# Hybrid mLSTM / neighbourhood-attention encoder: absorbed factors gathered per head, first two tiles transposed in the projection's loop, three column blocks behind the mLSTM

## The chip, the cores and the metric

The kernel runs on one core of a Trainium2 chip. The metric is the device time of one execution in microseconds (us). Engines are named as in the profile: PE is TensorE (PEld its weight loads), DVE is VectorE, ACT is ScalarE, POOL is GpSimd, SP is SyncE, which here only issues DMAs. Each engine works through its own queue in order; a waiting instruction holds up what is queued behind it on that engine.

## The reference

One encoder layer on 1024 tokens of width 1024, all in float32, with three residual sub-layers. It is cut here to what the changed stages compute.

```python
ALPHA = 2 ** 0.25
h = layer_norm(x, ln_in_w, ln_in_b)

# (1) token mixer: bidirectional mLSTM (4 heads x 128) beside neighbourhood attention (8 heads x 64)
z = h @ w_in + b_in
y = concat([mlstm(z), neighbourhood_attention(z)])
h = layer_norm(ALPHA * h + y @ w_mix_out + b_mix_out, ln1_w, ln1_b)

# (2) cross-attention, 4 heads of 256, into 256 memory tokens
q = h @ w_q;  k, v = split(mem @ w_kv)
p = softmax(q_head @ k_head.T / 16)          # per head
h = layer_norm(ALPHA * h + concat(p @ v_head) @ w_o + b_o, ln2_w, ln2_b)

# (3) ConvFFN: up-projection, width-3 depthwise conv, GELU gate, down-projection
h = layer_norm(ALPHA * h + conv_ffn(h), ln3_w, ln3_b)
```

## The kernel before

The program is written in Python against a tile library: tiles come from pools in on-chip memory, a pool that closes hands its room to the next one, and the library adds all waits between engines. A planner orders the instructions of each engine from its own forecast of durations: what stands earlier in the program goes first if it is ready, and later work is pulled forward into gaps. The order so found is fixed at build time. `tc.issue_after(x)` keeps an instruction behind `x` on its engine. Float32 products are done as three products of split operands (`mm3`, lines 223 to 225): a high and a low part, either `fp32r` (`split`, lines 228 and 229) or scaled `f16` (`split16`, lines 202 and 203). Every weight therefore passes a raw buffer (tag `wraw`, two buffers), a high part by ACT (tag `whi`, five buffers) and a low part by DVE or POOL (tag `wlo`, five buffers).

The stages, in order, with the lines and names that matter below:

- **Token projection** (`tok_chunk`), in the pools `w1` and `survey`.
- **Memory projection and absorbed factors** (pool `mem`, lines 486 to 560). The transposed memory is loaded in two halves through `wraw` and split into `memTh` and `memTl`; 16 weight pieces (line 126) give `xk` and `xv`. Then the query weights are multiplied into the keys and the output weights into the values, head by head, so that cross-attention needs no query and no output projection: `kq` = w_q times k, `vo` = v times w_o. The stream `wq` loads two weight rows of 512 KB per head, 16 in all, two ahead. Even ones are split by ACT and DVE, odd ones by ACT (line 136) and POOL (lines 137 and 138). Each head's result is four blocks of 128 x 512 in PSUM; `stage` evicts one (lines 202 and 203) into one of four small tiles and stores its high and its low half by one transfer each (line 533).
- **Column blocks** (`col_gen`): 16 weight pieces times two halves of the tokens, 24 matmuls each. The first 16 blocks run ahead of the mLSTM.
- **mLSTM** (`ml_gen`), eight chunks. The other 16 blocks (the queries and keys of neighbourhood attention) are mixed into it: `mix` runs `ml_gen`, adds up the costs that it yields, and takes the next filler while the filler's share done is below the main part's. The call is `mix(tc, anchor, ml_gen(), 48.3, cg, 15, 3)`: the main part's total, the filler's total, and a lag of three steps. One block is taken ahead of the call. The tokens' transposes lie in `X1` (first half) and `X2`, and blocks read both.
- **Neighbourhood attention** (`na_gen`), with the first half of the output projection (`out_half`, tiles named `fill`) as its filler. The mLSTM's result comes back through `wraw` (line 811) and is split into `X1`; the attention's goes into `X2`.
- **Second half of the output projection** (`out_half` with bank `out`, pool `wkB`), eight tiles of 128 tokens in order 0 to 7. After each, `after1` does the layer norm (`ln_tile`), and the tile is stored to `h1_d`. In `ln_tile` a tile's statistics are held behind the previous tile's product with the norm's weight (line 254).
- **Cross-attention** (pool `wkC`): tiles in the order `todo` = 0, 2, 1, 3, 4, 6, 5, 7 are loaded again (`load_r`), transposed (`to_hT`, line 1073) and split into `h1T`; then `scores`, softmax, `to_PT`, `out_d` and the norm. `to_B` transposes the result for the ConvFFN; `evict_wb` scales it out of PSUM, half on ACT (line 955), half on DVE (line 957).
- **ConvFFN**: 22 units of up-projection, convolution and gate, then the down-projection.

Of the kernel before, what the change touches and what calls it, by code (L numbers as in the profile page):

```python
# [20 lines left out]
NT = 8  # L21
# [35 lines left out]
def encoder(ctx, tc, I, out):  # L57
# [73 lines left out]
    def wload16(src, a, b, s, pool=False):  # L131
        raw = wp.tile([128, WP], F32, name="wraw", tag="wraw", bufs=2)[:, :a * b]
# [147 lines left out]
    with ExitStack() as ca:  # L280

        yml = None
        with ExitStack() as cm:
# [202 lines left out]
            with ExitStack() as c2:  # L486
                mm = c2.enter_context(tc.tile_pool(name="mem", bufs=1, reuse_waits="tile"))
                mT = [mm.tile([128, 8, 256], F32R, name="memT" + n) for n in "hl"]
                for q in range(2):
                    raw = wp.tile([128, WP], F32, name="wraw", tag="wraw", bufs=2)[:, :1024].rearrange(  # L490
                        "p (k t) -> p k t", k=4)
                    S.dma_start(raw, I["memT"][:, q * 1024:(q + 1) * 1024].rearrange("p (k t) -> p k t", k=4))
                    split(*(m[:, 4 * q:4 * q + 4, :] for m in mT), raw)
# [10 lines left out]
                for j, name in enumerate(("xk", "xv")):  # L504
                    x = mm.tile([128, 8, 256], F32, name=name)
                    xs_.append(x)
                    for i in range(8):
# [13 lines left out]
                        if j == 1 and i > 1:  # L521
                            next(gg, None)

                wq = Stream([(I["w_xqT"][i * 128:i * 128 + 128], 1, 1024) for i in range(8)] +
                            [(I["w_xo"][i * 128:i * 128 + 128], 1, 1024) for i in range(8)], 2,
                            load=lambda a, b, c, e: wload16(a, b, c, swq if wq.n < 8 else sx, wq.n % 2))

                def stage(ps, dst, shape):
                    st = mm.tile([128, 2, 512], F16, name="stage", tag="stage", bufs=4)

                    split16(st[:, 0], st[:, 1], ps, 2.0 ** -23)
                    for n in range(2):
                        S.dma_start(dst(n), st[:, n].rearrange("p (a m) -> p a m", a=shape))

                for h in range(4):
                    w = [wq.get(2 * h), wq.get(2 * h + 1)]
                    xh, xl = pairs["xk"]
                    for j in range(4):
# [6 lines left out]
                        stage(ps, lambda n: kq_d[n, :, 2 * j:2 * j + 2, h * 256:h * 256 + 256], 2)  # L545
# [3 lines left out]
                for h in range(4):  # L549
                    w = [wq.get(8 + 2 * h), wq.get(9 + 2 * h)]  # L550
                    xh, xl = pairs["xv"]
                    for b in range(2):
                        m = slice(b * 128, b * 128 + 128)
                        for ch in range(2):
# [5 lines left out]
                            stage(ps, lambda n: vo_d[n, :, 2 * h + b:2 * h + b + 1, c], 1)  # L560
# [208 lines left out]
        def out_half(w, y, res, dst, work, name, after=None, bias=None, rbufs=3, early=False, alpha=ALPHA):  # L769
# [10 lines left out]

            load_r(0)
            yield 0
            for tt in range(NT):
                if tt + 1 < NT:
                    load_r(tt + 1)
                r = rs.pop(tt)
# [815 lines left out]
```

## Time and profile before

| | |
|---|---|
| median of 3 runs | 1666.44 us (1665.78 to 1666.67) |
| profiled execution | 1660.96 us, span 1659.2 us |
| busy share of the span | PE 91%, PEld 59%, DVE 58%, ACT 44%, POOL 35% |
| mean granted PE clock | 0.969 |
| DMA | 214.11 MB, mean 129 GB/s |

The span reaches from the first to the last instruction. In a row of the profile stand start, duration, engine, line of the kernel, operation, the tile written, an arrow and the tiles read, the shape and the count; brackets at its end give the idle time of the engine just before, and what ended it. Window rows give the busy time of each engine in a stretch of the span, then the clock granted to PE (1.00 is full speed) and the share of time in which the DMA engines were busy.

### The profile page before, as it was taken

How to read it: one execution, taken by the hardware profiler on the slowest of the kernel's cores; microseconds unless marked ns; L12 is line 12 of the kernel's file. 1: busy time of each engine (PE TensorE's matmuls, PEld its weight loads, DVE VectorE, ACT ScalarE, POOL GpSimd, SP SyncE). 2: the span in 40 equal slices, each digit the busy share in tenths (PEclk: the TensorE clock that was granted, in tenths of full speed). 3: DMA queues.
4: the chain of work that ended last, by engine and by line, in shares of the span. 5: the costliest groups of instructions: out<-in, count | busy, mean ns of one | idle time of the engine just before them, and what ended most of it. 6: DMA issues, size and time to landing. Idle time of an engine off the chain costs nothing.

```text
span 1659.2 us, 21607 instructions
## 1 busy us (share of the span) xinstructions
PE 1504.0 (91%) x8134; PEld 973.1 (59%) x8134; DVE 969.2 (58%) x1774; ACT 734.7 (44%) x1212; POOL 584.3 (35%) x389
## 2 busy tenths in 40 slices
PE   6999786799999589895999988999999999998998
PEld 6999774488888478784455543444444444443443
DVE  8433374213454568856345677878888886945333
ACT  3311354312443356641233456777777775712000
POOL 5312234521433357615111236444443430110443
PEclk9999898999999799997999999999999999999999
DMA  8254446521545464266000133233322241932121
GB/s 306 92 176 147 157 136 216 203 71 45 138 160 135 155 222 129 77 229 254 25 31 34 52 114 130 102 115 121 120 102 114 111 169 70 332 130 68 47 77 51
DMA packets 85384, 214.11 MB, mean 129 GB/s; under 512 B 8224, under 2 KB 33056, under 8 KB 81952
## 3 DMA queue, kind: packets, MB, share of 16 engines
q1 hardware_dynamic: 84992, 211.98, 36.8%
q8 instruction: 64, 1.05, 0.3%
q0 software_dynamic: 144, 0.49, 0.1%
q14 instruction: 40, 0.33, 0.1%
q10 hardware_dynamic: 144, 0.26, 0.0%
HBM read 161.75 MB, written 51.45 MB: 128 GB/s over the span
## 4 chain that ended last, share of the span: by engine, by line
PE 29%; DVE 11%; ACT 6%; DMA 3%; issue 1%; POOL 1%; SPq 0%; DVEq 0%; ACTq 0%
PE dn L224 5%; PE dn L225 5%; PE dn L223 5%; PE S L223 3%; PE S L224 3%; PE S L225 3%; DMA sv<-in_w_down_dram 3%; DVE cbuf L1299 2%; DVE cbuf L1300 2%; PE z L224 1%; PE z L225 1%; PE z L223 1%; ACT cbuf L1298 1%; ACT cbuf L1306 1%; DVE wlo L203 1%
## 5 line engine op out<-in xcount | busy, mean ns | idle before, releaser
L128 POOL TENSOR_TENSOR wlo<-wraw,whi 128x1024 fp32r<-128x1024 f32 (+1 forms) x38 | 91.3, 2407 | 198.9 <-ACT whi L127 176.0
L223 PE MATMUL dn<-whi,yp 128*128 128x512 f16 x336 | 126.9, 380 | 1.4 <-ACT whi L202 1.4
L224 PE MATMUL dn<-wlo,yp 128*128 128x512 f16 x336 | 127.7, 381 | 0.0
L225 PE MATMUL dn<-whi,yp 128*128 128x512 f16 x336 | 127.5, 380 | 0.0
L127 ACT ACTIVATE whi<-wraw 128x1024 fp32r<-128x1024 f32 (+1 forms) x52 | 54.9, 1060 | 148.8 <-PE tk L225 47.9
L1217 POOL TENSOR_TENSOR wraw<-ur 128x512 f32<-128x512 f32 x22 | 46.0, 2091 | 200.7 <-issue 187.4
L1299 DVE SCALAR_TENSOR_TENSOR cbuf<-C,wdw,cbuf 128x1024 f32<-128x1024 f32 x44 | 75.7, 1721 | 28.4 <-ACT cbuf L1298 28.3
L251 ACT ACTIVATE r<-r,lnrs 128x1024 f32<-128x1024 f32 x19 | 23.6, 1241 | 121.6 <-DVE lnrs L250 121.6
L1300 DVE SCALAR_TENSOR_TENSOR cbuf<-C,wdw,cbuf 128x1024 f32<-128x1024 f32 x44 | 70.5, 1602 | 1.2
L223 PE MATMUL S<-kq,h1T 128*128 128x512 f16 x128 | 49.5, 387 | 22.6 <-ACT h1T L202 22.6
L223 PEld LDWEIGHTS <-yp 128*128 128x128 f16 x352 | 34.5, 98 | 51.4 <-issue 10.4
L203 DVE SCALAR_TENSOR_TENSOR wlo<-wraw,sc,whi 128x1024 f16<-128x1024 f32 x29 | 43.5, 1521 | 31.4 <-ACT whi L202 31.3
L224 PEld LDWEIGHTS <-yp 128*128 128x128 f16 x352 | 34.6, 98 | 41.9 <-issue 0.8
L225 PEld LDWEIGHTS <-yp 128*128 128x128 f16 x352 | 34.5, 98 | 41.9 <-issue 0.8
L1298 ACT ACTIVATE cbuf<-C,bdw,wdw 128x1024 f32<-128x1024 f32 x44 | 54.5, 1238 | 10.0 <-DVE C L1335 9.0
L1075 POOL TENSOR_TENSOR r<-r,vec 128x1024 f32<-128x1024 f32 x8 | 18.8, 2348 | 113.1 <-PE tp L1073 113.1
L202 ACT ACTIVATE whi<-wraw,sc 128x1024 f16<-128x1024 f32 x29 | 32.4, 1142 | 58.6 <-PE dn L225 33.3
L223 PE MATMUL tk<-whi,X1h 128*128 128x256 f32 (+1 forms) x192 | 55.9, 292 | 1.6 <-DVE ev L335 0.6
L223 PE MATMUL tk<-whi,X2h 128*128 128x256 f32 (+1 forms) x192 | 54.7, 285 | 1.4 <-DVE V L330 1.4
L225 PE MATMUL tk<-whi,X1l 128*128 128x256 f32 (+1 forms) x192 | 55.4, 290 | 0.4 <-DVE lnrs L240 0.4
L224 PE MATMUL tk<-wlo,X1h 128*128 128x256 f32 (+1 forms) x192 | 55.3, 289 | 0.0
L225 PE MATMUL tk<-whi,X2l 128*128 128x256 f32 (+1 forms) x192 | 54.7, 285 | 0.0
(449 smaller groups left out, 4866.4 us busy)
## 6 DMA issues: line engine op xcount, KB each, us to landing
ur<-in_w_up_dram SPq DMA_DIRECT2D x22, 1024.0 KB
sv<-in_w_down_dram SPq DMA_DIRECT2D x22, 512.0 KB
y<-cbuf SPq DMA_DIRECT2D x22, 512.0 KB
ur<-y SPq DMA_DIRECT2D x11, 1024.0 KB
wraw<-in_w_down_dram SPq DMA_DIRECT2D x22, 512.0 KB
r<-h SPq DMA_DIRECT2D x19, 512.0 KB
wraw<-in_w_col_dram SPq DMA_DIRECT2D x16, 512.0 KB
h<-r SPq DMA_DIRECT2D x16, 512.0 KB
```

The source lines that it names most:

```text
L127: A.activation(hi[:, :n], r3, AF.Copy)
L128: (eng or G).tensor_tensor(lo[:, :n], r3, hi[:, :n].bitcast(F32), OP.subtract)
L202: A.activation(hi, src, AF.Copy, scale=s)
L203: return V.scalar_tensor_tensor(lo, src, s, hi, op0=OP.mult, op1=OP.subtract)
L223: T.matmul(ps, lh, rh, start=first, stop=False, skip_group_check=skip)
L224: T.matmul(ps, lh, rl, start=False, stop=False, skip_group_check=skip)
L225: return T.matmul(ps, ll, rh, start=False, stop=last, skip_group_check=skip)
L251: A.activation(r, r, AF.Identity, scale=rs[:, 0:1], bias=rs[:, 1:2])
L1217: G.tensor_tensor(S1, A21, A22, OP.add)
L1298: A.activation(c, C[:, 1:SEQ + 1], AF.Identity, scale=wdw[:, 1, j:j + 1], bias=bdw[:, j:j + 1])
L1299: V.scalar_tensor_tensor(c, C[:, 0:SEQ], wdw[:, 0, j:j + 1], c, op0=OP.mult, op1=OP.add)
L1300: V.scalar_tensor_tensor(c, C[:, 2:SEQ + 2], wdw[:, 2, j:j + 1], c, op0=OP.mult, op1=OP.add)
```

## The change

It has five parts.

1. The memory is loaded by one transfer of 1 MB into a tile of its own, which takes the slot of `xv`. Odd rows of `wq` get raw tiles of their own (`wr`, two buffers). `stage` becomes one tile per head with both halves of all four blocks, in the slots of `memTh` and `memTl` by turns; `evict` fills it, and two transfers of 512 KB store it.
2. The divisor of the filler in `mix` goes from 15 to 12.
3. `out_half` takes an order of tiles, and the second half uses `todo`. The pool `wkC` opens ahead of the loop, and `to_hT` is called in `after1`: for the first tile after the second one, for the second tile after the fifth. `load_r` starts with two tiles instead of three, and the sum with `bxo` stands with the load.
4. In `after1`, `ln_tile` is called without weight and bias, and both follow it; the next tile's statistics are now held behind the small instruction of line 250.
5. `evict_wb` does columns 0 to 5 on ACT instead of 0 to 3.

```diff
-                mT = [mm.tile([128, 8, 256], F32R, name="memT" + n) for n in "hl"]
+                mT = [mm.tile([128, 8, 256], F32R, name="memT" + n, tag="memT" + n) for n in "hl"]
+                raw = mm.tile([128, 8, 256], F32, name="memraw", tag="xv")
+                S.dma_start(raw, I["memT"].rearrange("p (k t) -> p k t", k=8))
                 for q in range(2):
-                    raw = wp.tile([128, WP], F32, name="wraw", tag="wraw", bufs=2)[:, :1024].rearrange(
-                        "p (k t) -> p k t", k=4)
-                    S.dma_start(raw, I["memT"][:, q * 1024:(q + 1) * 1024].rearrange("p (k t) -> p k t", k=4))
-                    split(*(m[:, 4 * q:4 * q + 4, :] for m in mT), raw)
+                    split(*(m[:, 4 * q:4 * q + 4, :] for m in mT), raw[:, 4 * q:4 * q + 4, :])
...
+                def load(a, b, c, e):
+                    n = wq.n
+                    raw = None
+                    if n % 2:
+                        raw = mm.tile([128, 1024], F32, name="wr", tag="wr", bufs=2)
+                    return wload16(a, b, c, swq if n < 8 else sx, n % 2, raw)
...
-                def stage(ps, dst, shape):
-                    st = mm.tile([128, 2, 512], F16, name="stage", tag="stage", bufs=4)
-
-                    split16(st[:, 0], st[:, 1], ps, 2.0 ** -23)
-                    for n in range(2):
-                        S.dma_start(dst(n), st[:, n].rearrange("p (a m) -> p a m", a=shape))
+                def stage(h):
+
+                    t_ = "memT" + "hl"[h % 2]
+                    return mm.tile([128, 4096], F16, name="stage", tag=t_).rearrange("p (n x) -> p n x", n=2)
+
+                def evict(st, i, ps):
+
+                    split16(st[:, 0, i * 512:i * 512 + 512], st[:, 1, i * 512:i * 512 + 512], ps, 2.0 ** -23)
...
-                        stage(ps, lambda n: kq_d[n, :, 2 * j:2 * j + 2, h * 256:h * 256 + 256], 2)
+                        evict(st, j, ps)
+                    for n in range(2):
+                        S.dma_start(kq_d[n, :, :, h * 256:h * 256 + 256], st[:, n].rearrange("p (k m) -> p k m", k=8))
...
-                            stage(ps, lambda n: vo_d[n, :, 2 * h + b:2 * h + b + 1, c], 1)
+                            evict(st, 2 * b + ch, ps)
+                    for n in range(2):
+                        S.dma_start(vo_d[n, :, 2 * h:2 * h + 2], st[:, n].rearrange("p (b c) -> p b c", b=2))
...
-            mix(tc, anchor, ml_gen(), 48.3, cg, 15, 3)
+            mix(tc, anchor, ml_gen(), 48.3, cg, 12, 3)
...
-            if q == 0:
+            if q == 0 or i < 6:
...
             def after1(tt, r):
-                holds.append(ln_tile(r, lw, lb, small, hold=holds[-1] if holds else None))
+                holds.append(ln_tile(r, None, None, small, hold=holds[-1] if holds else None))
+                V.tensor_tensor(r, r, lw, OP.mult)
+                G.tensor_tensor(r, r, lb, OP.add)
                 S.dma_start(h1_d[tt * 128:(tt + 1) * 128, :], r)
+                if tt in todo[:2]:
+                    first.append(r)
+                    if tt == todo[1]:
+                        to_hT(ck, 0, first[0])
+                if tt == todo[4]:
+                    to_hT(ck, 1, first[1])
                 yield 1
 
-            run(out_half(wB, ylk(yna), part0_d, None, wk, "out", after1, rbufs=5))
+            first = []
+            run(out_half(wB, ylk(yna), part0_d, None, wk, "out", after1, rbufs=5, todo=todo))
...
-            for n in range(3):
-                load_r(n)
-            to_hT(ck, 0)
-            P = scores(ck, 0)
-            to_hT(ck, 1)
-            for n in range(NT):
-                Pn = scores(ck, n + 1) if n + 1 < NT else None
-                to_PT(P, n)
-                P = Pn
-                if n + 2 < NT:
-                    load_r(n + 3)
-                    to_hT(ck, n + 2)
-                if 0 < n < NT - 1:
-                    run(out_d(n - 1))
+        for n in range(2):
+            load_r(n)
+            G.tensor_tensor(rs[n], rs[n], bxo, OP.add)
+        P = scores(ck, 0)
+        for n in range(NT):
+            Pn = scores(ck, n + 1) if n + 1 < NT else None
+            to_PT(P, n)
+            P = Pn
+            if n + 2 < NT:
+                load_r(n + 2)
+                to_hT(ck, n + 2, rs[n + 2])
+                G.tensor_tensor(rs[n + 2], rs[n + 2], bxo, OP.add)
+            if 0 < n < NT - 1:
+                run(out_d(n - 1))
+        cC.close()
```

More of the change, by code (lines that the diff above doesn't have):

```diff
@@ L537, in encoder @@
                     xh, xl = pairs["xk"]
+                    st = stage(h)
                     for j in range(4):
@@ L767, in out_w, with out_half @@
                     for k in range(4)]
-        def out_half(w, y, res, dst, work, name, after=None, bias=None, rbufs=3, early=False, alpha=ALPHA):
+        def out_half(w, y, res, dst, work, name, after=None, bias=None, rbufs=3, early=False, alpha=ALPHA, todo=range(NT)):
             rs = {}
```

53 lines of the change are left out of this document (26 added, 27 removed).

## The prediction

> **What bounds the kernel now.** I read the page first, then TensorE's list of waits, then a table of stages, and last the rows of the stages that the change touches.
>
> ```profile
> span 1659.2 us, 21607 instructions
> PE 1504.0 (91%) x8134; PEld 973.1 (59%) x8134; DVE 969.2 (58%) x1774; ACT 734.7 (44%) x1212; POOL 584.3 (35%) x389
> ```
>
> TensorE is busy for 91% of the span; what is left to win without removing matmuls is the 155 us in which it idles, plus what it runs at half clock. The list of TensorE's waits (engine, line and what it waited for: us in total, times, longest) says where:
>
> ```profile
> PE S L223 <- ACT h1T L202: 22.6, 2, 22.3
> PE tp L755 <- DVE hm L752: 12.6, 5, 7.6
> PE fill L223 <- DVE wraw L796: 10.8, 1, 10.8
> PE mem L223 <- ACT whi L127: 8.9, 5, 6.6
> PE mem L223 <- DVE stage L203: 7.0, 7, 2.6
> PE mx L181 <- DVE am L1184: 6.0, 14, 1.3
> ```
>
> One wait of 22.3 us stands ahead of the first score matmul, two of 7.6 and 10.8 us behind the mLSTM, one of 6.6 us ahead of the memory projection, and many small ones in the absorbed-factor stage. The table of windows puts a stage around each:
>
> ```profile
> core 0: us, PE busy (x) PEld busy (x) DVE busy (x) ACT busy (x) POOL busy (x), PEclk, DMA share, GB/s
> 235.20:317.00 81.80, 56.13 (x320) 33.58 (x319) 35.98 (x54) 37.39 (x55) 42.97 (x17) 0.92 0.59 193
> 417.00:555.20 138.20, 132.10 (x780) 115.17 (x779) 67.45 (x258) 59.13 (x160) 50.09 (x42) 1.00 0.50 144
> 555.20:586.50 31.30, 8.99 (x28) 6.05 (x27) 14.14 (x31) 8.79 (x18) 11.88 (x16) 0.67 0.46 156
> 739.00:768.00 29.00, 28.67 (x132) 23.62 (x130) 20.90 (x46) 4.98 (x4) 10.98 (x8) 1.00 0.37 135
> 768.00:790.00 22.00, 0.06 (x1) 0.06 (x2) 11.97 (x23) 5.76 (x6) 12.10 (x9) 0.56 0.87 323
> 790.00:977.00 187.00, 186.40 (x936) 94.78 (x937) 94.66 (x211) 68.39 (x147) 35.06 (x23) 0.99 0.12 46
> 1100.00:1400.00 300.00, 294.04 (x1365) 131.85 (x1364) 237.64 (x269) 214.51 (x250) 110.46 (x56) 1.00 0.31 114
> ```
>
> In order: absorbed factors, mLSTM, its tail up to the first neighbourhood score, second half of the output projection, the hole behind it, cross-attention, and part of the ConvFFN. In 81.8 us of the absorbed factors no engine is full, nor are the DMA engines (0.59): a stage held by latency. The tail and the hole are nearly empty. Cross-attention is full, so what is won ahead of it shows at the end.
>
> **Absorbed factors (lines 523 to 560).** The slow part is the odd weights' way through the raw buffer. One round, from SP's, ACT's and POOL's rows:
>
> ```profile
> 253.60 0.82 SPq L134 DMA_DIRECT2D wraw<-in_w_xqT_dram  x2
> ...
> 256.82 1.15 ACT L136 ACTIVATE whi<-wraw,sc 128x1024 f16<-128x1024 f32 x1 [0.45 <-DMA wraw<-in_w_xqT_dram]
> ...
> 258.06 2.85 POOL L137 TENSOR_SCALAR wraw<-wraw,sc 128x1024 f32<-128x1024 f32 x1 [5.57 <-DMA wraw<-in_w_xqT_dram]
> 260.99 2.12 POOL L138 TENSOR_TENSOR wlo<-wraw,whi 128x1024 f16<-128x1024 f32 x1
> ...
> 264.22 0.34 SPq L134 DMA_DIRECT2D wraw<-in_w_xqT_dram  x1
> ```
>
> Load issued at 253.60, landed by 256.82, POOL done at 263.11, next load of that buffer at 264.22: 10.6 us a pair, and eight pairs are 85 us, about the stage. The change gives the odd weights two raw buffers of their own, so a load need not wait for POOL. A pair's floor is then the busiest resource: POOL 2.85 + 2.12 = 4.97 us, the DMA engines 0.59 x 81.8 / 8 = 6.0 us. Eight pairs at 6.0 are 48 us. In-order queues won't keep that engine full; I take 80%, so 60 us, a gain of 22. One end is the floor (gain 34). The other is no gain: the gathered tile has two homes (the slots of memTh and memTl) and leaves only with its last quarter, so head h+2 cannot evict before both stores of head h have been read. What that wait will cost no row shows; today nearly nothing waits on stores.
>
> ```profile
> L202 ACT ACTIVATE stage<-mem x32: 577/590/607, 243.9 to 318.9; 128x512 f16<-128x512 f32 x32
> L533 SPq DMA_DIRECT2D kq<-stage x32: 359/378/497, 245.8 to 282.6; - x32
> L203 DVE SCALAR_TENSOR_TENSOR stage<-mem,stage x32: 680/691/693, 246.5 to 319.5; 128x512 f16<-128x512 f32 x32
> L533 SPq DMA_DIRECT2D vo<-stage x32: 319/392/438, 285.5 to 320.4; - x32
> ```
>
> The 64 evictions stay as they are. The 64 store issues of about 0.385 us (24.6 us of SP's queue) become 16, each moved behind its head's last eviction; weight loads queue behind them on SP, but fewer times. I cost that at nothing: the two other heads' loads in flight hide it.
>
> A rule speaks against the full gain. VectorE's and POOL's rows:
>
> ```profile
> 251.30 2.27 DVE L203 SCALAR_TENSOR_TENSOR wlo<-wraw,sc,whi 128x1024 f16<-128x1024 f32 x1
> ...
> 250.37 2.12 POOL L138 TENSOR_TENSOR wlo<-wraw,whi 128x1024 f16<-128x1024 f32 x1
> ```
>
> VectorE's split began under POOL's instruction and ended 1.08 us after it. The Trainium skill (SBUF — State Buffer, Who interferes with whom) says that a VectorE instruction with two SBUF inputs and a GpSimd instruction that reads SBUF exclude each other for a whole instruction. By that rule POOL's 4.97 us and VectorE's split would add up in every pair instead of overlapping; in a tighter stage I would price it at some 3 us, and the sum below would be 3 us less of a gain. The row agrees for this one instruction; whether it reaches TensorE no run here shows yet.
>
> **memT.** Its load leaves the raw buffer for one 1 MB transfer into the slot of xv.
>
> ```profile
> 170.54 1.99 ACT L228 ACTIVATE memTh<-wraw 128x1024 fp32r<-128x1024 f32 x2
> ...
> 960.64 1.21 SPq L1176 DMA_DIRECT2D ur<-in_w_up_dram  x2
> ...
> 966.03 1.28 POOL L1217 TENSOR_TENSOR wraw<-ur 128x512 f32<-128x512 f32 x1 [7.36 <-DMA ur<-in_w_up_dram]
> ```
>
> Today memT's split stands at 170.54, at the end of the projection, and the weights' loads follow it. After, weights come early, but memT's room lies in a pool that reuses the projection's. If that is free early, the 6.6 us wait and a half-clock stretch go (gain 7.5). If only at the end, 1 MB lands 5.4 us after its issue (960.64 to 966.03), no sooner than today's weights: a loss of up to 2. The first write at 170.54 is nearest to the late case; with the weights' later waits gone (8.9 less 6.6) I take a gain of 1.5.
>
> **Column blocks.** The fill's divisor goes from 15 to 12. A block is 5.73 us of TensorE:
>
> ```profile
> 522.75:528.48 5.73, 5.73 (x29) 4.76 (x28) 3.51 (x15) 2.34 (x5) 2.62 (x2) 1.00 0.91 128
> ...
> 570.93 0.37 SPq L811 DMA_DIRECT2D wraw<-yml  x1
> ...
> 586.51 0.58 PE L223 MATMUL S<-kh,qsh 128*128 128x256 f32 x1 [2.70 <-ACT kh L885]
> ```
>
> With the yields of ml_gen (51.2 in all against 48.3) the thirteenth block comes behind chunk 7's last num matmul and the last two behind everything: three blocks, 17.2 us, leave the mLSTM, which TensorE bounds (132.1 of 138.2 us). They run where TensorE does 9 of 31.3 us. With less filling the mLSTM's own waits grow (6.1 us idle now; I take 3 more), so chunk 7 ends 14 us earlier. Its chain (norm, store, the yml load of 570.93, split, first keys, 586.51) is 31.3 us today and moves with it. What is late next is X1: block 14 holds it until about 553, and four splits follow. I take 13 us. Ends: 19 (all three blocks and half-clock time) and 3 (the splits go one after another through a single raw buffer).
>
> **First two tiles.** Today the first h1T waits for all eight norms:
>
> ```profile
> 787.93 1.24 ACT L251 ACTIVATE r<-r,lnrs 128x1024 f32<-128x1024 f32 x1 [4.47 <-DVE lnrs L250]
> 789.20 1.27 ACT L202 ACTIVATE h1T<-tp,sc 128x512 f16<-128x512 f32 x2
> ...
> 789.94:802.70 12.76, 12.76 (x50) 5.39 (x51) 3.52 (x8) 1.73 (x5) 2.35 (x1) 0.82 0.11 42
> 803.96:814.40 10.44, 10.44 (x49) 4.82 (x50) 3.12 (x7) 1.61 (x5) 2.09 (x1) 1.00 0.00 0
> ```
>
> After, both transposes, their splits and their tiles stand in the loop, in a pool opened ahead of it, and scores may start when the projection's matmuls end at 768. That closes the 22.3 us and the half-clock loss (12.76 against 10.44). The transposes themselves only move. The hold moves from the weight's product to the small factor's instruction, so the next tile's statistics go ahead of that product. Prices: two transposes now stand in TensorE's order between matmuls and wait there for their tile, as the hm transposes do ((12.6 - 7.6) / 4 = 1.25 us each); the last tiles' norms fall beside the first scores, whose softmax is needed a whole score block (10.4 us) later; the loads of Vo on SP are needed some 21 us after 768, and today's burst (0.87 of the engines) is over by 790. I take 21 us; ends 24.5, and 10 if scores still wait for half of the norms. The bias's sums on POOL and the loads of r are as many as before and hidden.
>
> **Eviction.** Two of VectorE's four scalings per tile go to ScalarE.
>
> ```profile
> 985.21 1.04 DVE L957 TENSOR_SCALAR r<-tp,wb 128x128 f32<-128x128 f32 x3
> ...
> 980.42 0.80 ACT L955 ACTIVATE r<-tp,wb 128x128 f32<-128x128 f32 x2
> ```
>
> 0.35 us each leaves VectorE, 0.40 comes to ScalarE. Under full TensorE it is hidden; at the last two tiles it moves the end by at most 2 x 0.7 us either way. I take 0.
>
> **Sum.** 22 + 1.5 + 13 + 21 = 57.5 us. The profiled execution took 1660.96 us (span 1659.2 and 1.76 around it), so 1603.5; the median shown, 1666.44, is 5.5 longer, and the forecast in its terms is **1609**.
>
> **Rivals.** (1) *The gathered tile becomes the wait.* The stage keeps its 82 us, VectorE and ScalarE waiting for stores. For it: two homes and release only at the head's end. Against: 1.0 MB a head at the stage's 193 GB/s is 5 us, less than a head. Time: 1609 + 22 = 1631. (2) *The mLSTM is held by its own chain.* Blocks leave, chunk 7 ends 4 us earlier, X1 comes free at 563. For it: five waits on hm. Against: TensorE's 96% there. Gain 3 instead of 13: 1619. (3) *The stores cost the DMA engines half of their time.* Fewer, larger ones lower that floor; POOL's 8 x 4.97 = 40 us and some 6 to fill remain, so 46: 1609 - 14 = 1595. Against: no row shows a wait of TensorE for a store. The Trainium skill (DMA: Bandwidth & Descriptors, Rules for kernel authors) speaks for it with its advice to coalesce many small transfers into a large one. (4) *Slower: the ConvFFN slips.* All queues are written from one planner's forecast, and an earlier start may order its 22 units worse. Today TensorE waits 14 times for am there, 0.43 us each, with VectorE at 238 of 300 us: little slack. At the longest wait seen (1.3 us) 20 units lose 26 us; from 57.5 / 20 = 2.9 us a unit on, the kernel is slower than before. At 3.2 us: 1609 + 64 = 1673. Against: nothing in that stage is edited.
>
> **Numbers.** Forecast 0.62, own range 1594 to 1626; rival (1) 0.15, (2) 0.10, (3) 0.08, (4) 0.05. The range of 8 in 10 takes in (1) and (3) and leaves out (4) and the tails: 1588 to 1636. A change of this kernel under 0.2% (3.3 us) cannot be told from none: faster 0.92, same 0.03, slower 0.05.
>
> **What would show it.** Absorbed stage near 60 us with odd weights' loads issued while POOL works; waits on stage stores if (1). Three full blocks between chunk 7's last num and the first neighbourhood score, that score some 13 us nearer to the mLSTM's start. No wait over 3 us ahead of the first scores, two transposes among the projection's matmuls. ConvFFN's window as long as now. A gap at any of these places as long as today's, or a new one in a stage that isn't edited, makes the prediction wrong.

## The result and the profile after

The changed kernel takes 1605.97 us (median of four runs, 1604.28 to 1608.26) against 1666.56 us (1665.78 to 1670.93): a ratio of 0.9632, interval 0.961 to 0.9654. The profiled execution took 1604.78 us (span 1603.1), 56.2 us less than that of before. The medians lie 60.6 us apart, because the profiled execution of before was 5.6 us under its median and that of after 1.2 us. The page of the changed kernel:

```profile
span 1603.1 us, 21461 instructions
...
PE 1496.0 (93%) x8134; PEld 970.6 (61%) x8134; DVE 968.4 (60%) x1758; ACT 739.9 (46%) x1228; POOL 585.7 (37%) x389
```

TensorE's busy time fell by only 8 us, with the mean granted clock at 0.979 instead of 0.969; the other 48 us are idle time that went. The list of TensorE's waits after:

```profile
PE mem L224 <- ACT memTh L229: 10.2, 1, 10.2
PE fill L224 <- DVE wraw L810: 8.6, 1, 8.6
PE dn L224 <- ACT yp L203: 8.0, 1, 8.0
PE z L224 <- ACT TX1l L1083: 7.0, 1, 7.0
PE mx L182 <- DVE am L1207: 5.9, 14, 1.3
```

The 22.3 us for h1T are gone, and the small waits for stage and hm are no longer among the longest. The wait ahead of the memory projection did not go: it is 10.2 us where it was 6.6, and for another tile. A wait of 7.0 us at the start of the ConvFFN (ahead of a `z` matmul) is new. The am wait is as it was.

Where the time went is read from the first and last matmul of each group. TensorE's groups of before (columns: count, duration min/median/max in ns, first and last start in us, shape):

```profile
L223 PE MATMUL mem<-memTh,whi x128: 274/281/580, 177.3 to 238.2; 128*128 128x256 f32 x128
...
L225 PE MATMUL mem<-whi,xvl x32: 377/379/631, 273.0 to 316.1; 128*128 128x512 f16 x32
```

```profile
L714 PE MATMUL num<-V,whi x128: 271/275/315, 419.7 to 554.9; 128*128 128x129 f32 x128
```

And of after:

```profile
L224 PE MATMUL mem<-memTh,whi x128: 274/281/584, 183.8 to 247.7; 128*128 128x256 f32 x128
...
L226 PE MATMUL mem<-whi,xvl x32: 377/379/631, 268.2 to 297.2; 128*128 128x512 f16 x32
```

```profile
L728 PE MATMUL num<-V,whi x128: 271/275/378, 400.0 to 520.0; 128*128 128x129 f32 x128
```

Rows of the timeline after, and its windows (memory stages, tail, cross-attention, ConvFFN):

```profile
543.47 0.80 PE L224 MATMUL fill<-whi,X1h 128*128 128x512 f32 x1 [8.63 <-DVE wraw L810]
...
551.21 0.74 PE L224 MATMUL S<-kh,qsh 128*128 128x256 f32 x3 [2.31 <-ACT kh L899]
...
716.90 1.03 PE L996 MATMUL tp<-ident,r 128*128 128x128 f32 x8
...
723.25 1.03 PE L996 MATMUL tp<-ident,r 128*128 128x128 f32 x8
...
732.98 0.39 PE L226 MATMUL out<-whi,X2l 128*128 128x512 f32 x1
733.21 0.39 PE L224 MATMUL S<-kq,h1T 128*128 128x512 f16 x1
```

```profile
183.85:297.50 113.65, 101.82 (x697) 81.40 (x698) 69.35 (x120) 58.85 (x86) 62.10 (x24) 0.93 0.55 183
...
520.00:551.20 31.20, 20.27 (x81) 15.79 (x79) 16.93 (x28) 11.44 (x19) 16.42 (x17) 0.84 0.59 207
733.20:924.90 191.70, 185.28 (x936) 93.83 (x935) 107.70 (x222) 77.83 (x162) 45.62 (x32) 1.00 0.23 85
1050.00:1350.00 300.00, 291.19 (x1349) 130.25 (x1348) 237.03 (x275) 217.76 (x251) 105.19 (x54) 1.00 0.30 110
```

Both transposes stand among the projection's matmuls without a wait in brackets, and the first score matmul follows the last projection matmul after 0.23 us. In the tail TensorE now works for 20.3 of 31.2 us (9.0 of 31.3 before). Cut at these points (starts of matmuls), the profiled executions differ as follows (us; the second stretch holds the memory projection and the absorbed factors, and the recorded expectations, which count it to the end of its last matmul, give 139.2 and 113.7 for it):

| stretch | before | after | change | forecast |
|---|---|---|---|---|
| to the first memory matmul | 177.3 | 183.8 | +6.5 | -1.5 |
| from there to the last one (memory and absorbed factors) | 138.8 | 113.4 | -25.4 | -22 |
| to the last num matmul (mLSTM) | 238.8 | 222.8 | -16.0 | |
| to the first neighbourhood score (tail) | 31.6 | 31.2 | -0.4 | -13 for both |
| to the first cross-attention score | 203.4 | 182.0 | -21.4 | -21 |
| to the first up-projection matmul (z) | 190.1 | 191.7 | +1.6 | 0 |
| to the end | 679.1 | 678.2 | -0.9 | 0 |

How many of the column blocks' matmuls (tile `cl`, 24 a block) moved can be counted. Behind the last num matmul (520.0) stand 50 of them, where none stood before the change: two blocks and the last two matmuls of a third. Three blocks end there, as the prediction and the expectations below have it, but 22 matmuls of the first of them still stand ahead, among those of chunk 7.

### The profile page after: what moved, and what is told of

It reads as the page before. It is cut to its first block, busy times and chain, and to the rows that moved or that the text cites. A ratio compares the mean times of both kernels' runs of the same rounds, so it can differ in the third digit from the quotient of the medians.

```text
span 1603.1 us, 21461 instructions
## 1 busy us (share of the span) xinstructions
PE 1496.0 (93%) x8134; PEld 970.6 (61%) x8134; DVE 968.4 (60%) x1758; ACT 739.9 (46%) x1228; POOL 585.7 (37%) x389
## 4 chain that ended last, share of the span: by engine, by line
PE 38%; DVE 15%; ACT 8%; DMA 7%; issue 3%; POOL 1%; SPq 1%; DVEq 0%; ACTq 0%; POOLq 0%
PE dn L225 5%; PE dn L226 5%; PE dn L224 5%; PE S L224 3%; PE S L225 3%; PE S L226 3%; DMA sv<-in_w_down_dram 3%; DVE cbuf L1322 3%; DVE cbuf L1323 2%; PE z L225 2%; PE z L226 2%; PE z L224 2%; DVE wlo L204 1%; ACT cbuf L1321 1%; DVE unitYh L204 1%
## 5 line engine op out<-in xcount | busy, mean ns | idle before, releaser
L242 POOL TENSOR_TENSOR lnrs<-lnrs,mhalf 128x1 f32<-128x1 f32 x32 | 23.0, 719 | 99.0 <-DVE lnrs L241 84.0
L224 PE MATMUL tk<-whi,X1h 128*128 128x256 f32 (+1 forms) x192 | 55.8, 292 | 2.3 <-DVE V L331 0.9
L225 PE MATMUL tk<-wlo,X2h 128*128 128x256 f32 (+1 forms) x192 | 54.7, 285 | 0.0
```

The source lines that it names most:

```text
L224: T.matmul(ps, lh, rh, start=first, stop=False, skip_group_check=skip)
L225: T.matmul(ps, lh, rl, start=False, stop=False, skip_group_check=skip)
```

## The experiments

Each run is one profiled execution cut at the same points; the medians are of 4 or 5 runs, and each ratio is to runs of the kernel before on the same chip.

| run | to first mem | memory and absorbed | mLSTM | tail | first score to z | median | ratio, interval |
|---|---|---|---|---|---|---|---|
| changed kernel | 183.8 | 113.4 | 222.8 | 31.2 | 373.7 | 1605.97 | 0.9632, 0.961 to 0.9654 |
| memT in halves | 181.5 | 113.7 | 228.1 | 31.1 | 374.5 | 1603.92 | 0.962, 0.9595 to 0.9645 |
| no own raw | 183.8 | 138.6 | 224.0 | 31.2 | 379.5 | 1635.44 | 0.9802, 0.977 to 0.9833 |
| block stores | 182.8 | 113.7 | 222.7 | 31.1 | 380.0 | 1608.91 | 0.9651, 0.9622 to 0.9679 |
| divisor 15 | 183.6 | 114.5 | 239.2 | 31.6 | 374.9 | 1620.31 | 0.971, 0.9676 to 0.9743 |
| first tiles behind | 183.0 | 111.4 | 224.5 | 31.1 | 402.9 | 1633.12 | 0.9791, 0.977 to 0.9812 |
| old hold | 184.5 | 112.1 | 229.5 | 31.2 | 374.5 | 1603.55 | 0.9617, 0.9592 to 0.9642 |
| one own raw | 183.6 | 139.9 | 224.3 | 31.1 | 376.2 | 1636.68 | 0.9814, 0.9792 to 0.9835 |
| order of last blocks | 187.5 | 114.2 | 223.5 | 32.1 | 373.9 | 1609.3 | 0.9638, 0.9617 to 0.9658 |
| divisor 11 | 184.3 | 112.7 | 229.3 | 33.6 | 379.2 | 1615.19 | 0.9681, 0.9655 to 0.9708 |
| divisor 11, order | 184.0 | 110.7 | 227.3 | 33.3 | 379.1 | 1612.18 | 0.9666, 0.9642 to 0.969 |
| VectorE splits | 184.5 | 111.0 | 224.8 | 31.0 | 372.9 | 1606.49 | 0.963, 0.9604 to 0.9657 |
| memory first | 178.1 | 111.6 | 224.9 | 31.3 | 376.9 | 1602.66 | 0.9619, 0.9601 to 0.9636 |

The rows of stretches that an edit doesn't touch show how far single executions scatter: up to 7 us in the mLSTM (old hold, whose order of TensorE instructions there is that of the changed kernel) and in the stretch from score to z, 4 us ahead of the first memory matmul (order of last blocks). A difference of that size in one trace proves nothing by itself.

### The odd weights' raw buffers

Three runs take the absorbed factors apart. First, the odd rows go back to the common buffers:

```diff
-                    if n % 2:
-                        raw = mm.tile([128, 1024], F32, name="wr", tag="wr", bufs=2)
```

> The changed kernel, with the odd weight rows of the absorbed factors again in the common two raw buffers; the gathered tile and its large stores stay. Theory of the prediction: the own raw buffers carry this part's gain (the stretch from the first to the last matmul of the memory stages went from 139.2 to 113.7 us, 25.5 us less). Then the 10.6 us cycle of a pair returns, the stretch is 130 us or more, and the time is 1606 + 16 to 22 = 1622 to 1628. Rival: the gathered stores carry it (48 store issues fewer on SP's queue, 18 us of it); then the stretch stays within 5 us of 113.7, and the time is 1606 to 1611.

The whole gain is gone, though the gathered tile and its 16 large stores are still there. The group that ends the stage:

```profile
L226 PE MATMUL mem<-whi,xvl x32: 377/379/634, 278.6 to 322.4; 128*128 128x512 f16 x32
```

From 183.8 to 322.4 is 138.6 us, the 138.8 of before. The time is some 29 us above the changed kernel's, beyond the 16 to 22 expected (in this execution 5.8 us lie behind the first score, within the scatter). Second, the number of stores:

```diff
-                    for n in range(2):
-                        S.dma_start(kq_d[n, :, :, h * 256:h * 256 + 256], st[:, n]...)
+                        for n in range(2):
+                            S.dma_start(kq_d[n, :, 2 * j:2 * j + 2, h * 256:h * 256 + 256], st[:, n, j * 512:j * 512 + 512]...)
...
```

(shortened: each block is stored when it is evicted, and `vo` likewise)

> The changed kernel, with the gathered tile and the own raw buffers, but with each block of it stored when it is evicted: 64 stores instead of 16. Theory of the prediction: the number of stores costs nothing, the two loads in flight hide it; the time stays within 4 us of 1606. Rival: SP's queue is what the weights' loads wait for; 48 issues of 0.385 us more are 18.5 us of that queue, and with half of it on the path the time is some 1615, with all of it 1624.

With 64 stores the stretch is 113.7 us, as with 16. The windows of the same 47 us, first with block stores, then in the changed kernel, show the price on the DMA engines (column before last: 0.88 and 0.83); the stretch is no longer for it:

```profile
250.00:297.00 47.00, 38.47 (x225) 22.32 (x222) 32.03 (x44) 29.17 (x43) 37.93 (x14) 0.96 0.88 270
```

```profile
250.00:297.00 47.00, 40.41 (x244) 24.12 (x243) 32.70 (x46) 31.17 (x46) 36.61 (x14) 0.96 0.83 279
```

The medians are 3 us apart with overlapping intervals. Third, one own raw tile instead of two, which tells the cycle from the mere separation:

```diff
-                        raw = mm.tile([128, 1024], F32, name="wr", tag="wr", bufs=2)
+                        raw = mm.tile([128, 1024], F32, name="wr", tag="wr", bufs=1)
```

> The changed kernel with one raw tile of their own for the odd weight rows instead of two. Theory of the cycle: a raw buffer is taken from its load's issue until POOL is done with it, some 9.5 to 10.6 us; with one own buffer a pair of rows still takes that long, so the stretch from the first to the last matmul of the memory stages goes back from 113.7 to some 130 to 139 us and the time to 1622 to 1631. Rival: it is enough that the odd rows no longer share their buffer with the even ones (and with the weights of other stages); then one tile brings most of the gain, and the time is 1606 to 1614.

The stretch is 139.9 us: one buffer gives nothing. The rows of the own raw tile in this run (issues on SP's queue; then what POOL's instructions on it waited for, us and times) say why,

```profile
L135 SPq DMA_DIRECT2D wr<-in_w_xo_dram x4: 332/332/333, 276.8 to 312.3; - x4
...
  ACT whi L137: 39.7, 7
```

and the same row of the changed kernel:

```profile
L135 SPq DMA_DIRECT2D wr<-in_w_xo_dram x4: 433/1142/1636, 259.1 to 279.3; - x4
```

Four loads of odd value weights are issued in 35.5 us, 11.8 us apart, with one tile, and in 20.2 us, 6.7 us apart, with two. With one, POOL idles 39.7 us for ACT's high half, which has to wait for the next load. What bounded the stage before the change was how many odd loads may be in flight; whether a third tile would bring more was not tried. The gathered tile's part in this may be room: by their shapes the four old tiles took 4 x 2 KB of each partition, and the two raw tiles take 2 x 4 KB. No run keeps the old tiles beside the raw ones.

### memT

```diff
-                raw = mm.tile([128, 8, 256], F32, name="memraw", tag="xv")
-                S.dma_start(raw, I["memT"].rearrange("p (k t) -> p k t", k=8))
                 for q in range(2):
+                    raw = wp.tile([128, WP], F32, name="wraw", tag="wraw", bufs=2)...
+                    S.dma_start(raw, I["memT"][:, q * 1024:(q + 1) * 1024]...)
...
```

> The changed kernel, with the memory loaded as before, in two halves through the common raw buffers. Theory: in the changed kernel the one 1 MB load is issued only at 175.99 us, and TensorE waits 10.15 us until 183.85 for its first memory-projection matmul (177.35 before); the halves come at 125 us, so this wait falls back to some 4 to 6.6 us and the time falls by 4 to 7 us, from 1606 to about 1600. Rival A: the weights' loads behind are what holds the stage, so the end of the absorbed factors stays where it is and the time stays within 2 us of 1606. Rival B: the raw buffers that the halves take up delay the projection's own weights, and the time rises by some 3 us to 1609.

The theory fails: the first matmul moved by 2.3 us only, still behind a wait of 9.13 us, and the medians cannot be told apart. Rival A is nearest: TensorE now waits for the high part of a key weight, and the last memory matmul starts at 295.2 instead of 297.2. In the changed kernel the load stands late on SP's queue, behind two key weights, and 6.75 us pass from its issue to its first use:

```profile
173.95 1.42 SPq L126 DMA_DIRECT2D wraw<-in_w_xk_dram  x2
175.61 0.33 SPq L343 DMA_DIRECT2D mo<-ev  x1
175.99 0.42 SPq L491 DMA_DIRECT2D memraw<-in_memT_dram  x1
...
182.74 2.00 ACT L229 ACTIVATE memTh<-memraw 128x1024 fp32r<-128x1024 f32 x2 [9.20 <-DMA memraw<-in_memT_dram]
```

With the halves, another wait took its place. SP's and TensorE's rows of this run:

```profile
173.50 0.87 SPq L135 DMA_DIRECT2D wr<-in_w_xqT_dram  x2
174.48 11.06 SPq L126 DMA_DIRECT2D wraw<-in_w_xk_dram  x4
...
181.53 0.58 PE L224 MATMUL mem<-memTh,whi 128*128 128x256 f32 x1 [9.13 <-ACT whi L127]
```

Two loads of 512 KB into the free own raw tiles, which are needed late, went out ahead of the first key weight (in the changed kernel their first use is at 230.7). The last run holds them back, and makes the odd rows' low halves by VectorE (see below):

```diff
...
-                    return wload16(a, b, c, swq if n < 8 else sx, n % 2, raw)
+                    with tc.issue_after(issued[n0 + 7].ins):
+                        return wload16(a, b, c, swq if n < 8 else sx, False, raw)
...
```

(shortened: `issued` collects the loads of the weights, `issued[n0 + 7]` is that of the eighth key weight; the memory's halves are as above)

> The changed kernel with three edits ahead of the mLSTM: the memory in two halves through the common raw buffers, as before the change; the loads into the odd rows' own raw tiles held behind the load of the eighth key weight, so that they no longer stand ahead of the key weights on SP's queue; and the low halves of the odd rows made by VectorE. Theory: with the halves alone the first memory-projection matmul moved only from 183.85 to 181.53 us, because two loads into the own raw tiles were issued at 173.50, ahead of the first key weights (174.48); with these behind, it stands at 177 to 178.5, the stretch to the last memory matmul stays at 111 to 114 us, and the time falls by 5 to 8 us against the changed kernel, from 1606 to 1598 to 1601. Rival: the weights' loads themselves set the stage, whatever goes first; then the stretch grows by what the start gained, the last memory matmul stays at 295 to 297 us and the time at 1604 to 1607.

```profile
173.59 16.26 SPq L128 DMA_DIRECT2D wraw<-in_w_xk_dram  x6
...
178.07 0.58 PE L226 MATMUL mem<-memTh,whi 128*128 128x256 f32 x1 [6.56 <-ACT whi L129]
```

The first matmul stands at 178.07 and the wait is 6.56 us, as before the change; the stretch stays at 111.6. This is the fastest profiled execution of all (span 1599.1). Its median, 1602.66 us, is 3.3 us under the changed kernel's; the intervals overlap (0.9601 to 0.9636 against 0.961 to 0.9654), so the trace shows the gain at its place, and the medians do not yet settle its size.

### The first two tiles

```diff
-                if tt in todo[:2]:
-                    first.append(r)
-                    if tt == todo[1]:
-                        to_hT(ck, 0, first[0])
-                if tt == todo[4]:
-                    to_hT(ck, 1, first[1])
...
         for n in range(2):
             load_r(n)
+            to_hT(ck, n, rs[n])
             G.tensor_tensor(rs[n], rs[n], bxo, OP.add)
```

> The changed kernel with the transposes of the first two tiles moved out of the projection's loop again, behind it; the order of tiles and the shorter hold of the norms stay. Theory of the prediction: the place in the loop carries this part's 21.5 us; the hole ahead of the first scores returns with a wait of 18 to 22 us, and the time is 1606 + 18 to 22 = 1624 to 1628. Rival: the shorter hold of the norms and the new order carry half of it; the wait is 10 us or less, and the time is 1616 or less.

The hole returns, and larger than expected and than before the change (33.2 us; 18 to 22 were expected, 22.3 before). TensorE's, POOL's and SP's rows:

```profile
762.56 1.97 PE L996 MATMUL tp<-ident,r 128*128 128x128 f32 x8 [33.20 <-DMA r<-h]
```

```profile
741.72 2.34 POOL L1024 TENSOR_TENSOR r<-r,vec 128x1024 f32<-128x1024 f32 x1 [2.86 <-DVE lnrs L241]
744.02 0.55 POOL L242 TENSOR_TENSOR lnrs<-lnrs,mhalf 128x1 f32<-128x1 f32 x1
747.43 2.34 POOL L1024 TENSOR_TENSOR r<-r,vec 128x1024 f32<-128x1024 f32 x1 [2.86 <-DVE lnrs L241]
```

```profile
738.38 17.44 SPq L1025 DMA_DIRECT2D h<-r  x4
758.29 2.46 SPq L1092 DMA_DIRECT2D r<-h  x5
```

Four tiles are not normalised when the projection ends at 729; each takes 5.7 us (741.72 to 747.43), and the load of the first tile waits on SP behind the stores of all four, until 758.29. With the transposes in the loop the first scores need neither those stores nor that load: the tiles are taken where they lie, and the late norms run beneath the scores. The run moves two things at once, the place of the transposes and the tile they read (the one loaded again instead of the one in the loop); which of them carries how much, and why the hole is longer than before the change, was not tried. The new order of tiles is kept in every run, so its share is not known either. The shorter hold does not close the hole in this run, and with the transposes in the loop it gives nothing:

```diff
-                holds.append(ln_tile(r, None, None, small, hold=holds[-1] if holds else None))
-                V.tensor_tensor(r, r, lw, OP.mult)
-                G.tensor_tensor(r, r, lb, OP.add)
+                holds.append(ln_tile(r, lw, lb, small, hold=holds[-1] if holds else None))
```

> The changed kernel with the layer norm of the projection's loop as before: weight and bias inside it, the next tile's statistics held behind the product with the weight. Theory: with the first two tiles transposed in the loop no score waits for the last norms, so the hold costs nothing: 1604 to 1609. Rival: each tile's chain of norm instructions is what lets the scores start without a wait; with eight products of about 1.2 us in the chain again, the later tiles come late, and the time rises by 5 to 10 us to 1611 to 1616.

Score to z takes 374.5 against 373.7 us, the time is not distinguishable.

### The column blocks

```diff
-            mix(tc, anchor, ml_gen(), 48.3, cg, 12, 3)
+            mix(tc, anchor, ml_gen(), 48.3, cg, 15, 3)
```

> The changed kernel with the filler's divisor back at 15. Theory: three blocks of 5.73 us return into the mLSTM and the hole behind it opens again; chunk 7's last num matmul and the first neighbourhood score come 15 to 17 us later, and the time is 1621 to 1623. Rival: the mLSTM is held by its own chain, the blocks take little of it; the time is 1610 or less.

As the theory has it: the mLSTM takes 16.4 us more, the tail stays at 31.6 us, the time rises by 14.3 us. But it is two blocks that return into that stretch (no `cl` matmul is left behind the last num matmul, 50 in the changed kernel). The same with divisor 11 instead of 12:

> The changed kernel with the filler's divisor at 11 instead of 12. Theory: from chunk 7's last num matmul to the first neighbourhood score it takes 31.2 us with three blocks behind the mLSTM (520.0 to 551.2) as with none (554.9 to 586.5 before), and TensorE works for only 20.3 of them; a fourth block, 5.73 us, still fits, that distance stays at 31 to 32 us, and the time falls by some 5 us, from 1606 to 1601. Rival: X1 is what is late; the fourth block holds X1 for 5.73 us more, the splits into X1 move behind it, the distance grows to 36 or 37 us and the time stays at 1605 to 1607.5.

Neither: it is slower by 9 us. The tail grew by 2.4 us, not 5.7, and the mLSTM, with a block less in it (73 `cl` matmuls behind its last num matmul, 50 at divisor 12), took 229.3 us instead of 222.8 (217 if the block had simply left). The waits of TensorE in the mLSTM, first of the changed kernel, then with divisor 11, and the windows of both in that order:

```profile
PE tp L769 <- DVE hm L766: 1.7, 3, 0.7
PE num L728 <- ACT hm L740: 0.2, 1, 0.2
```

```profile
PE tp L769 <- DVE hm L766: 8.3, 4, 2.5
PE num L728 <- ACT hm L740: 1.5, 3, 1.0
```

```profile
400.00:520.00 120.00, 118.04 (x716) 103.55 (x715) 64.69 (x260) 54.92 (x154) 46.55 (x41) 1.00 0.52 150
```

```profile
399.90:526.30 126.40, 116.32 (x693) 101.82 (x692) 62.88 (x259) 55.21 (x154) 46.89 (x41) 0.97 0.49 142
```

23 matmuls fewer save only 1.7 us of TensorE's time (118.04 to 116.32), with the granted clock at 0.97, and 8 us of idle time are new. One trace does not prove this, for the run with the old hold took 229.5 us in the mLSTM with the changed kernel's order and divisor 12:

```profile
PE tp L769 <- DVE hm L766: 5.7, 3, 3.4
399.80:526.10 126.30, 119.75 (x715) 105.09 (x714) 66.96 (x260) 54.86 (x154) 47.00 (x41) 0.99 0.50 142
```

All runs together say more. From the last memory matmul to the last num matmul TensorE idles 1.7 to 6.6 us in the ten runs with divisor 12, and 10.1 and 8.2 us in the two with 11; with 15 it idles 5.8 us, and 6.5 before the change. So the waits do grow with the block that leaves at 11. That this block had been filling the waits for hm fits, but no run changes those waits alone. Another 5.5 us of this execution lie between the first score and z, as in runs that touch neither (block stores). Two orders test X1 as the limit:

```diff
-[(i, hf) for p in range(4) for i in (8 + p, 12 + p) for hf in range(2)]
+[(i, hf) for p in range(3) for i in (8 + p, 12 + p) for hf in range(2)] + [(11, 0), (15, 0), (11, 1), (15, 1)]
```

> The changed kernel with the last four column blocks in another order, so that the last block that reads X1 is the second but one from the end's third place: (11, first half), (15, first half), (11, second half), (15, second half). Theory: in the changed kernel the hole behind the mLSTM (531.7 to 551.2 us, TensorE busy for 8.6 of 19.5) is set by X1, which the last blocks hold; its first splits stand at 529.3, behind the last block that reads it. With X1 free one block of 5.73 us earlier the splits and the loads behind them go beneath the last block, and the first neighbourhood score comes 3 to 6 us earlier: 1600 to 1603. Rival: the chain of chunk 7 (transposes at 531.47, store at 533.00, load at 535.63) and the last key load (544.92) set the hole; then nothing moves by more than 2 us: 1604 to 1608.

> The changed kernel with the divisor at 11 and the last four blocks in the order (11, first half), (15, first half), (11, second half), (15, second half), so that the last two read only X2. Theory of the rival of the run with divisor 11 alone, X1: with X1 free one block earlier the splits stand where they stand in the changed kernel, the distance from the last num matmul to the first neighbourhood score stays at 31 to 32 us, and the time is some 1601, 5 us under the run with the old order. Other theory, the chain of chunk 7 alone sets that distance: the order makes no difference, both runs with divisor 11 come within 2 us of each other.

With divisor 12 the tail is 32.1 us, not shorter. The order did free X1 earlier: its last reader stands 0.4 us behind the last num matmul instead of 5.8 us. But the first split into X1 starts 7.8 us behind that matmul as against 8.2, so X1 is not what holds it. With divisor 11 the first split moves from 11.4 to 7.6 us behind the last num matmul, and the tail changes by 0.3 us only (33.6 to 33.3), as the theory of the chain has it; the medians are 3 us apart with overlapping intervals, where that theory allowed 2. Neither run reaches the 1601 us that the theories of X1 or of a free fourth block asked for: both are slower than the changed kernel.

### VectorE and POOL side by side

```diff
-                    return wload16(a, b, c, swq if n < 8 else sx, n % 2, raw)
+                    return wload16(a, b, c, swq if n < 8 else sx, False, raw)
...
-            if q == 0 or i < 6:
+            if q == 0:
```

> The changed kernel with two edits in different stages, read by stage. First, VectorE instead of POOL makes the low halves of the odd weight rows (one instruction of 1.3 to 2.9 us instead of 2.85 and 2.12 us on POOL). If VectorE's and POOL's instructions with operands in SBUF hold each other up, as the rows of 2.03 and 2.88 us for VectorE's split and of 3.82 and 3.14 us for POOL's suggest, VectorE's split falls back to 1.28 us everywhere, and the stretch from the first to the last matmul of the memory stages goes from 113.4 to about 107 to 110 us; the raw tile comes free 3.7 us earlier per row. Rival: VectorE becomes the bound or the stretch is held by the stores and loads (DMA engines at 0.81); it stays at 112 to 118. Second, the eviction for the ConvFFN goes back to half of it on ACT: by the prediction nothing, the stretch from the first neighbourhood score to the first up-projection matmul stays within 2 us of 373.7. Time by the theory 1600 to 1604, by the rival 1605 to 1611.

VectorE's split of a weight row in the changed kernel, and in this run:

```profile
L204 DVE SCALAR_TENSOR_TENSOR wlo<-wraw,sc,whi x8: 1266/1731/2877, 231.4 to 285.3; 128x1024 f16<-128x1024 f32 x8
```

```profile
L204 DVE SCALAR_TENSOR_TENSOR wlo<-wraw,sc,whi x8: 1266/1276/1285, 232.3 to 278.1; 128x1024 f16<-128x1024 f32 x8
L204 DVE SCALAR_TENSOR_TENSOR wlo<-wr,sc,whi x8: 1268/1282/1286, 234.1 to 280.8; 128x1024 f16<-128x1024 f32 x8
```

Without POOL's instructions on the odd rows all 16 take 1.27 to 1.29 us; beside them eight took up to 2.88. The rows of the changed kernel show the other side, too:

```profile
261.48 3.14 POOL L139 TENSOR_TENSOR wlo<-wr,whi 128x1024 f16<-128x1024 f32 x1
```

```profile
260.16 2.48 DVE L204 SCALAR_TENSOR_TENSOR xvl<-xv,sc,xvh 128x1024 f16<-128x1024 f32 x2
```

POOL's 2.12 us became 3.14 while VectorE's pair ran until 262.64, 1.16 us into it. That agrees with the rule of the Trainium skill (SBUF — State Buffer, Who interferes with whom) that a VectorE instruction with two SBUF inputs and a GpSimd instruction that reads SBUF exclude each other for whole instructions. What it costs TensorE cannot be told from nothing: the stretch is 111.0 instead of 113.4 us, but it is 110.7 to 114.5 us in the six other runs that leave this stage as the changed kernel has it, and the time is the same.

The eviction's split makes no difference to the length either: 372.9 against 373.7 us from the first score to z. But it is what the new wait of 7.0 us hangs on. In the twelve runs with six columns on ACT TensorE waits 6.2 to 7.4 us there; with half of them on ACT again, in this run:

```profile
PE z L224 <- ACT TX1l L1083: 3.0, 1, 3.0
```

Smaller waits stand beside it, as before the change. In sum little changes: of the first 55 us behind the first z matmul TensorE idles 10.2 us in the changed kernel, 11.9 of 55.8 in this run and 10.0 of 55.1 before the change.

## Why the prediction was right, point by point

**The sum.** Forecast -57.5 against the profiled execution, measured -56.2. Two errors nearly cancel: memT was 8.0 us worse than forecast, absorbed factors and blocks 6.8 us better together. That the sum comes so close is luck; that each of the three large gains is there, at its place, is not.

**Absorbed factors (-22 forecast, -25.4 found).** The mechanism holds: two raw buffers carry all of it, one carries nothing, the stores nothing. The size was low, and the term is the share of 80% at which the floor of 48 us was to be reached. It shows best with the memory in halves, where the absorbed products hardly mix with the memory's: from the first to the last of them it takes 56.4 us (238.8 to 295.2), where 60 were forecast and 80.9 were needed before (235.2 to 316.1). In the changed kernel the same products take 66.4 us (230.8 to 297.2), because memory products until 248.0 stand among them; the whole stretch is as long either way (113.7 and 113.4). Rival (1), the gathered tile as the wait, came only in small: ScalarE waited 2.4 us in all for stores of kq, and TensorE's waits for stage add up to 2.2 us. Rival (3), the stores' price, is out by the run with 64 of them. The advice of the Trainium skill (DMA: Bandwidth & Descriptors, Rules for kernel authors) to coalesce, named in that rival's favour, brings no time here: without it the DMA engines were 0.05 busier and the stretch was as long.

**memT (-1.5 forecast, +6.5 found).** This step failed, outside its own range of -7.5 to +2, and not by scatter: all eleven runs with this load have their first memory matmul at 182.8 to 187.5, against 177.3 before. The step priced the load's landing (5.4 us, found 6.75) but not its place on SP's queue: it was issued at 175.99, behind two key weights. The profile shows no wait of the load itself there; whether its room would have been free earlier, as the step asked, was not tried. Of the 6.5 us, 3.6 are a longer wait (10.15 against 6.56). The other 2.9 lie ahead of it: the last projection products end that much later (the mx matmuls stand at 173.21, at 170.30 before), for a reason that was not tried. The weights did come early, as forecast (the first at 125.02); nothing could use them.

**Column blocks (-13 forecast, -16.4 found).** The gain is there, but the terms that made it up were wrong. Little more than two blocks left the mLSTM, not three: TensorE's work from the last memory to the last num matmul fell by 11.4 us (231.9 to 220.5), not by 17.2. And the waits, priced at 3 us more, became 4.6 us less (6.5 to 2.0 us of idle time). That the two errors cancel is luck, and the second is not firm: the idle time of this stretch is 1.7 to 6.6 us over the runs with divisor 12. X1, named as what is late next, did not lengthen the tail. Rival (2), the mLSTM held by its own chain, did not come at divisor 12; longer waits inside the mLSTM, of its kind, appear one block later, at 11.

**First two tiles (-21 forecast, -21.4 found).** By the steps named: the scores start with the end of the projection, at a granted clock of 1.00. The price of 1.25 us for each set of transposes did not fall due: neither waits. The hold's part is nothing that the runs can show.

**Eviction and ConvFFN (0 forecast).** In time as said; rival (4) did not come (am waits 5.9 us, 6.0 before), and the stretch from z to the end is 0.9 us shorter. The prediction did not see the new wait of 7.0 us, and by its last sentence a new gap in a stage that is not edited would have made it wrong. This one goes with the edited eviction, as the run without that edit shows, and it lies where several smaller ones stood.

## What to carry to other kernels

A load that is read late in a long split needs as many raw buffers as rounds that must overlap (here two, where one gave nothing): read the cycle of one buffer from its load's issue to the next issue, and do not expect a gain from a buffer that only separates two streams. When a load is moved into a tile of its own, look at its place on the issuing queue, both behind what stands there and ahead of what it passes: a tile that is free early lets loads that nobody needs go first. Filler moved behind a stage is won until the stage's own waits grow; the next block then costs more than it brings. Count in the trace how much of the filler has moved, before its price is compared with the gain.

## What was not expected of the hardware

One fewer block in the mLSTM did not make it shorter: with divisor 11 it took 229.3 and 227.3 us in two runs, where the ten runs with divisor 12 took 222.7 to 229.5. In the run without the new order, 8.3 us of short waits for hm came with a granted clock of 0.97 in place of 1.00 over 126 us, so that 23 matmuls fewer gave back only 1.7 us of TensorE time. And POOL, too, is held up by VectorE beside it (3.14 us for an instruction of 2.12), where the prediction had seen only VectorE's side.
